# FFN ends of a two-layer encoder: the next norm's first rows turned by a DMA, product 2's weights kept for product 3, one activation split moved

## The chip, the core and the metric

The kernel runs on one core of a Trainium2 chip. The engines that it uses are TensorE (PE; its weight loads are PEld), VectorE (DVE), ScalarE (ACT), GpSimd (POOL) and SyncE (SP). SP issues the plain and the transposing DMAs, POOL the accumulating ones; each engine works through its own queue in order. The metric is the device time of one execution in microseconds (us).

## The reference

A residual stream x of 512 tokens by 1024 features in float32 goes through two layers and a last norm:

```python
for l in range(DEPTH):      # 2
    x = x + 0.5 * swiglu(rms_norm(x, ffn1_norm[l]), ffn1_w_in[l], ffn1_w_out[l])
    x = x + mixer(rms_norm(x, mix_norm[l]), mix_w_in[l], ...)
    x = x + 0.5 * swiglu(rms_norm(x, ffn2_norm[l]), ffn2_w_in[l], ffn2_w_out[l])
return rms_norm(x, final_norm)

def rms_norm(x, g): return x * rsqrt(mean(x * x, -1) + 1e-6) * g
def swiglu(x, w_in, w_out):
    g, u = split(x @ w_in, 2, axis=-1)      # w_in 1024 x 5632
    return (silu(g) * u) @ w_out            # w_out 2816 x 1024
```

The mixer (neighbourhood attention beside a 2-D Fourier transform, gated) is not touched by the change. There are four FFNs: FFN1 and FFN2 of layer 0, FFN1 and FFN2 of layer 1. Their ends, in order of time, are called ends 1 to 4. The last one is followed by the final norm and not by another stage.

## The kernel before

**Products.** Every large product is done by one level of Strassen's scheme: both matrices are cut into 2 by 2 blocks, and seven products of sums of blocks, numbered 1 to 7, take the place of eight. Each float32 operand is split into a high part of reduced precision (type fp32r) and the rest, its low part, and each term of a product is three matmuls in `product` and `granule`: high weights by high activations (L508), high by low (L509), low by high (L511). One matmul takes a 128x128 weight block against 128x512 values.

**Weights.** They come from memory as granules of 128 x 1024 float32 (512 KB; 256 KB for 128 x 512). `Raw.load` issues one load on SP (L148); where a granule is a sum of two blocks, POOL adds a second one in place by an accumulating DMA (L150). The granules lie in a pool of 9 buffers. On the chip each is split: ScalarE copies it to `whi` (L186 or L191), VectorE subtracts that from it to give `wlo` (L187 or L194), three buffers of each. `Stream` runs over the list of all granules in order of use: loads are issued up to 8 items ahead of the split (`FETCH`), the split is made 2 items ahead of its use (`AHEAD`). Product 3 needs the sum of blocks d and b: its item loads d, with its accumulate, and b again, and VectorE adds the two (`Item.summed`, L164) ahead of the split.

**The body of an FFN** (`stage_ffn`) does gate and up products over five blocks of the hidden features. A block does products 1, 5, 6, 2, 7, 3 and 4 in that order into the PSUM tiles A, B and C. From them come two halves of gated values, z2 and then z1 (z2 before product 4, z1 behind it). They have tokens on the partitions and must be turned: `halves` calls `apart`, in which ScalarE makes two copies that separate the 16-bit words of z (tile `zs`, L346) and SP issues one transposing DMA to tile `zt` (L347). Later ScalarE joins the words again (`joined_words`, L356), two instructions per z, into the activation tiles `at`. For the last block that happens inside the FFN end.

**The FFN end** is the loop over `steps`: 21 short products against the output weights, i = 0 to 20, each over one of three chunks c of hidden features. Product 1 is i = 0 to 2, product 2 is i = 3 to 5, then chunk by chunk products 5, 6, 7 and 3 (i = 6 to 17), and product 4 (i = 18 to 20). Chunk 0 has three blocks of 128 hidden features per half (18 matmuls), chunks 1 and 2 have four (24 matmuls). `make(i)` splits the activations of step i: for product m, ScalarE makes the tile `c<m>h` and VectorE `c<m>l` (L321, L322). The program calls `make` for steps i, i + 1 and i + 2 around step i. z1 of the last block is joined behind i = 2, z2 behind i = 5. Finished sums are added into x by VectorE (`update`, L756).

**The next norm** needs its rows of x turned and split into tiles `xh` and `xl` (two buffers each). For the first quarter, `nxt.quad(0, 0)` behind i = 6, TensorE transposes eight 128x128 blocks into PSUM (L413), ScalarE takes them out with the norm's gain (L416) and makes the high half (L417), and VectorE makes the low half (L418). From the end of the block loop, where the FFN's own norm tiles have had their last use, until those tiles are written anew, `xh` and `xl` lie unused. In end 4 (`late`) there is no next norm of this kind.

The order of the instructions in each engine's queue is laid out when the kernel is built, by a planner that works from the program's order and the engines' modelled loads; in a few places, around i = 18 among them, it is written out by hand (`manual_schedule`).

Of the kernel before, what the change touches and what calls it, by code (L numbers as in the profile page):

```python
# [9 lines left out]
F32 = mybir.dt.float32  # L10
# [3 lines left out]
U16 = mybir.dt.uint16  # L14
AF = mybir.ActivationFunctionType
# [3 lines left out]
P = 128  # L19
D = 1024  # L20
T = 512
# [16 lines left out]
NB = 5  # L38
# [52 lines left out]
def encoder_kernel(  # L91
# [45 lines left out]


    class Raw:
        def __init__(self, key, n=1024, plus=None):  # L140
            self.key, self.n, self.plus, self.t = key, n, plus, None

        def load(self, parts=1):
            if self.t is None:
                self.t = raw_pool[0](self.n)
                for c in range(0, self.n, self.n // parts):
                    cs = slice(c, c + self.n // parts)
                    nc.sync.dma_start(out=self.t[:, cs], in_=wst[GRAN_AT[self.key]][:, cs])  # L148
                if self.plus:
                    G.dma_start(out=self.t, in_=wst[GRAN_AT[self.plus]][:, 0 : self.n], accum_op=ALU.add)  # L150
# [48 lines left out]
    def stage_items():  # L199
        items, st = [], 0  # L200

        def add(*a, **k):
            items.append(Item(*a, stage=st, **k))

        def strassen(s, name, idx, sizes, order, dma=False, behind=None):
            def key(q, g):
                return (s, name(q), idx, g) if g < 2 else (s, "h" + q, idx, 0)

            r = {}
            for q, q2 in (("a", None), ("b", None), ("c", "a"), ("d", "c")):  # L210
                r[q] = [Raw(key(q, g), n, q2 and key(q2, g)) for g, n in enumerate(sizes)]
            d2 = [Raw(key("d", g), n) for g, n in enumerate(sizes)]
            at = [(m, g) for m in order for g in range(len(sizes))]
            if len(sizes) == 3:
                at.remove((2, 2))
                at.insert(at.index((7, 2)), (2, 2))
            for m, g in at:
                a, b, c, d = [r[q][g] for q in "abcd"]
                if m == 1:
                    add(a, neg=True)  # L220
                elif m == 2:
                    add(b)
                elif m == 3:
                    add(d, None if dma else b)
                elif m == 4:
                    add(d2[g])
                elif m == 5:
                    add(d)
                elif m == 6:
                    add(d, a, then=b.key if dma else None)  # L230
                else:
                    add(c)
                for key in (behind or {}).get(m, ()) if g == len(sizes) - 1 else ():
                    add(Raw(key))

        def out_sizes(c):
            return (1024, 512) if c == 0 else (1024, 1024)

        def ffn(s):
            first = not items  # L240
            if first:
                for g in range(4):
                    add(Raw((s, "cl", g)), parts=2 if g < 2 else 1, pieces=2 if g == 0 else 1)
            for j in range(NB):
                order = (1, 2, 5, 6, 7, 3, 4) if first and j == 0 else (1, 5, 6, 2, 7, 3, 4)
                strassen(s, lambda q: q, j, (1024,) * (2 if first or j else 3), order)
            for order in ((1,), (2,), (5, 6, 7, 3), (4,)):
                for c in range(3):
                    strassen(s, lambda q: "o" + q, c, out_sizes(c), order)

        for l in range(L):
            ffn((l, 1))
            st += 1
# [12 lines left out]
            for g in range(2):  # L266
                add(Raw((s, "n", 1, g)))
            strassen(s, lambda q: "w" + q, 0, two, ORDER, True)
            ffn((l, 2))
        return items  # L270

    class Stream:
# [6 lines left out]
        def fetch(self, to):  # L279
            n = len(self.items)  # L280
            while self.loaded < min(to, n) and self.items[self.loaded].stage <= self.stage:
                self.items[self.loaded].load()
                self.loaded += 1

# [25 lines left out]

    ws = Stream()
    raw_pool = [None]

    def mm3(ps, lh, ll, rh, rl, start, stop, again=False):
        PE.matmul(ps, lh, rh, start=start, stop=False, skip_group_check=again)  # L315
# [15 lines left out]
    def rsqrt(ms, n):  # L331
# [6 lines left out]
            V.scalar_tensor_tensor(r, t, 1.5, r, ALU.add, ALU.mult)  # L338
        return r

    def apart(z):

        s, t = slot(U16, "zs", (2, 4, 2, P)), slot(U16, "zt", (2, 4, 256))
        words = z.bitcast(U16).rearrange("p b (q f h) -> p h q b f", q=4, h=2)
        for h in range(2):
            S.activation(s[:, h], words[:, h], AF.Copy)  # L346
        nc.sync.dma_start_transpose(  # L347
            out=t.rearrange("p h q (b t) -> p (h q b) t", b=2), in_=s.rearrange("p h q b f -> p (h q b f)")
        )
        return t  # L350

    def joined_words(to, t):

        to = to.bitcast(U16).rearrange("p i (t w) -> p w i t", w=2)
        for w in range(2):
            S.activation(to[:, w], t[:, w], AF.Copy)  # L356

    class Norm:
# [39 lines left out]

        def quad(self, i, j):
            self.quad_high(i, j)()  # L400

        def quad_high(self, i, j):

# [211 lines left out]
    def stage_ffn(norm, nxt, late):  # L615
# [77 lines left out]
        def halves(z, j, f0):  # L693

            turned.append((apart(z), j, f0))
# [175 lines left out]
        for jb in range(0 if first else 1, NB):  # L871
# [36 lines left out]
            z2 = gate(s2, 1)  # L908
            times(z2, [sb[:, 0, :], sb[:, 1, :]], 1)
            halves(z2, 1, f0)  # L910
            product(pa, acts[4], K4, False, again=True)
            times(z1, pa, 0)
            halves(z1, 0, f0)

        if late or nxt.mix:
            tc.keep_in_program_order(S.activation(small("sq", 1), ones, AF.Sqrt))
        ps = {}
        for i, (m, c, _) in enumerate(steps):
            make(i)
            if i:  # L920
# [1067 lines left out]
```

## Time and profile before

| | |
|---|---|
| three runs | 1858.85, 1858.40, 1857.83 us, median 1858.4 |
| profiled execution | 1859.64 us, span 1857.9 us |
| granted TensorE clock, mean | 0.999 |
| TensorE busy | 1842.2 us (99%), 8862 matmuls |
| VectorE busy | 1605.6 us (86%) |
| ScalarE busy | 1311.2 us (71%) |
| GpSimd busy | 171.3 us (9%) |
| DMA traffic | 394.21 MB, 212 GB/s over the span |
| SP's weight loads of 512 KB | 470, 5.7 us from issue to landing (median) |
| POOL's accumulates of 512 KB | 174, 8.0 us |
| SP's transposing DMAs | 44, 5.5 us |

In the lines below, a timeline row reads: start in us, length in us, engine, line of the kernel, operation, tile written <- tiles read, shape and type, count; in brackets the idle time of that engine before it and what ended it. Matmuls overlap, so the distance between starts, not the length, is what one costs.

### The profile page before, as it was taken

What the parts mean: (1) busy time and instruction counts of PE and PEld (TensorE: products, weight loads), DVE (VectorE), ACT (ScalarE), POOL (GpSimd) and SP (SyncE); (2) the same over time, 40 slices, a digit from 0 to 9 for tenths busy, and PEclk for the clock granted to TensorE, in tenths of its full rate; (3) what the DMA queues carried; (4) which work ended last, traced back from release to release, by engine and by line L of the source; (5) the groups of instructions that cost most, each with busy time, mean ns of one, the idle gap of its engine ahead of it and who ended that gap; (6) DMA issues with size and microseconds to landing.
All of it is one profiled execution on the core that took longest, in us unless ns stands there. A gap on an engine that the chain in (4) does not pass through costs nothing.

```text
span 1857.9 us, 24616 instructions
## 1 busy us (share of the span) xinstructions
PE 1842.2 (99%) x8862; PEld 1530.1 (82%) x8862; DVE 1605.6 (86%) x1950; ACT 1311.2 (71%) x1780; POOL 171.3 (9%) x210
## 2 busy tenths in 40 slices
PE   9999999999999999999999999999999999999997
PEld 7888878888888888888888888888888888888886
DVE  7878899786889987889998888998869899887898
ACT  6777875668676767777666778766675776777865
POOL 0001011100111010001010100101001101010010
PEclk9999999999999999999999999999999999999999
DMA  9898799932896788879888887988249867888794
GB/s 301 222 240 219 188 255 277 216 118 86 248 230 183 180 224 223 216 199 263 253 200 217 225 216 198 268 278 212 69 150 237 227 174 178 234 210 215 211 280 145
DMA packets 198458, 394.21 MB, mean 212 GB/s; under 512 B 103808, under 2 KB 103936, under 8 KB 198336
## 3 DMA queue, kind: packets, MB, share of 16 engines
q1 hardware_dynamic: 169664, 294.30, 49.2%
q0 software_dynamic: 28528, 98.33, 29.7%
q8 instruction: 69, 1.13, 0.3%
q14 instruction: 53, 0.43, 0.1%
q10 hardware_dynamic: 144, 0.02, 0.0%
HBM read 365.85 MB, written 2.11 MB: 198 GB/s over the span
## 4 chain that ended last, share of the span: by engine, by line
PE 88%; DVE 6%; DMA 2%; issue 2%; ACT 1%; SPq 0%; DVEq 0%; ACTq 0%
PE A L508 10%; PE A L511 10%; PE A L509 10%; PE B L509 5%; PE B L508 5%; PE B L511 5%; PE o L511 5%; PE o L509 5%; PE o L508 4%; PE ps L315 4%; PE ps L316 3%; PE ps L317 3%; PE C L508 3%; PE C L509 3%; PE C L511 3%
## 5 line engine op out<-in xcount | busy, mean ns | idle before, releaser
L194 DVE TENSOR_TENSOR wlo<-raw,whi 128x1024 fp32r<-128x1024 f32 (+1 forms) x534 | 632.0, 1195 | 172.8 <-ACT whi L191 171.3
L191 ACT ACTIVATE whi<-raw 128x1024 fp32r<-128x1024 f32 (+1 forms) x534 | 546.0, 1033 | 253.5 <-DVE raw L164 56.9
L150 POOL DMA_DIRECT2D raw<-in_wst_dram x166 | 144.2, 887 | 1339.3 <-DMA raw<-in_wst_dram 596.8
L164 DVE TENSOR_TENSOR raw<-raw,raw 128x1024 f32<-128x1024 f32 (+1 forms) x150 | 179.2, 1195 | 2.0
L509 PE MATMUL A<-whi,xl 128*128 128x512 f32 x400 | 155.7, 389 | 0.0
L508 PE MATMUL A<-whi,xh 128*128 128x512 f32 x400 | 155.7, 389 | 0.0
L356 ACT ACTIVATE at<-zt 128x1024 uint16<-128x1024 uint16 (+2 forms) x96 | 111.0, 1168 | 20.9 <-DMA zt<-zs 20.9
L186 ACT ACTIVATE whi<-raw 128x1024 fp32r<-128x1024 f32 (+1 forms) x83 | 85.9, 1035 | 46.9 <-issue 12.5
L511 PE MATMUL A<-wlo,xh 128*128 128x512 f32 x400 | 115.0, 389 | 0.0
L187 DVE SCALAR_TENSOR_TENSOR wlo<-raw,whi 128x1024 fp32r<-128x1024 f32 (+1 forms) x83 | 98.4, 1195 | 11.3 <-ACT whi L186 11.0
L511 PEld LDWEIGHTS A<-wlo,xh 128*128 128x128 f32 x400 | 75.1, 188 | 15.6
L508 PEld LDWEIGHTS A<-whi,xh 128*128 128x128 f32 x400 | 75.1, 188 | 15.4
L509 PEld LDWEIGHTS A<-whi,xl 128*128 128x128 f32 x400 | 75.1, 188 | 15.4
L508 PE MATMUL C<-whi,xh 128*128 128x512 f32 x208 | 81.1, 390 | 0.5 <-ACT whi L191 0.5
L509 PE MATMUL C<-whi,xl 128*128 128x512 f32 x208 | 81.0, 389 | 0.0
L509 PE MATMUL B<-whi,xl 128*128 128x512 f32 x208 | 81.0, 389 | 0.0
L508 PE MATMUL B<-whi,xh 128*128 128x512 f32 x208 | 80.9, 389 | 0.0
L730 ACT ACTIVATE th<-sn,rh 128x512 f32<-128x512 f32 x80 | 55.1, 715 | 36.2 <-DVE sn L583 35.4
L346 ACT ACTIVATE zs<-th 128x1024 uint16<-128x1024 uint16 x80 | 79.5, 1042 | 0.9 <-DVE th L737 0.9
L578 ACT ACTIVATE sn<-A 128x512 f32<-128x512 f32 x104 | 59.0, 584 | 24.9 <-PE A L511 24.9
L511 PE MATMUL B<-wlo,xh 128*128 128x512 f32 x208 | 59.8, 389 | 0.0
L511 PE MATMUL C<-wlo,xh 128*128 128x512 f32 x208 | 59.8, 389 | 0.0
(438 smaller groups left out, 4681.5 us busy)
## 6 DMA issues: line engine op xcount, KB each, us to landing
raw<-in_wst_dram SPq DMA_DIRECT2D x470, 512.0 KB, 5.7
raw<-in_wst_dram POOLq DMA_DIRECT2D x174, 512.0 KB, 8.0
raw<-in_wst_dram SPq DMA_DIRECT2D x30, 256.0 KB, 3.8
bm<-in_bias_dram SPq DMA_DIRECT2D x16, 384.0 KB, 3.5
x<-in_xin_dram SPq DMA_DIRECT2D x4, 512.0 KB, 10.2
raw<-in_wst_dram POOLq DMA_DIRECT2D x8, 256.0 KB, 8.4
dft<-in_dft_dram POOLq DMA_DIRECT2D x8, 256.0 KB, 4.3
gb<-in_gbias_dram SPq DMA_DIRECT2D x4, 512.0 KB, 14.8
```

The lines of the kernel that those rows point to most:

```text
L150: G.dma_start(out=self.t, in_=wst[GRAN_AT[self.plus]][:, 0 : self.n], accum_op=ALU.add)
L164: V.tensor_tensor(self.raw.t, self.raw.t, self.add.t, ALU.add)
L186: S.activation(hi, t, AF.Copy, scale=-1.0)
L187: self.last = V.scalar_tensor_tensor(lo, t, -1.0, hi.bitcast(F32), ALU.mult, ALU.subtract)
L191: S.activation(hi[:, cs], t[:, cs], AF.Copy)
L194: self.last = V.tensor_tensor(lo[:, cs], t[:, cs], hi[:, cs].bitcast(F32), ALU.subtract)
L315: PE.matmul(ps, lh, rh, start=start, stop=False, skip_group_check=again)
L346: S.activation(s[:, h], words[:, h], AF.Copy)
L356: S.activation(to[:, w], t[:, w], AF.Copy)
L508: PE.matmul(ps, lh, rh, start=start, stop=False, skip_group_check=again)
L509: PE.matmul(ps, ll, rh, start=False, stop=False, skip_group_check=again)
L511: PE.matmul(ps, lh, rl, start=False, stop=stop, skip_group_check=again)
```

## The change

It touches the four FFN ends in three ways.

1. Product 2's granules (block b) get a fixed home. They are loaded into `kept[0]` and `kept[1]`, which are two tiles of the tag `xh`, and `kept[2]`, one of tag `xl`, and the same data serve product 3, so b is not loaded a second time: five loads of 512 KB and one of 256 KB fewer per end, 24 loads over the kernel. The stream's loading stops at such an item until `homes[0]` is set behind the block loop. In the built order of SP's queue, the kept loads stand among the other loads around the last block's two transposing DMAs: between that of z2 and that of z1 there is one load of 512 KB in the kernel before, and there are two of 512 KB and one of 256 KB in the changed one. Kept tile 2 is one that the last block's product 3 reads last (its low activations), kept tile 0 another of product 3 (the high ones), kept tile 1 one that product 4 reads.
2. In ends 1 to 3, `nxt.quad(0, 0)` is replaced by the generator `turned_quad`, advanced one step behind each of i = 6, 8, 11, 12, 13, 14 and 15: two ScalarE copies of words of x into tile `words` (the other `xl` tile), a transposing DMA on SP, two joins, four scalings by the gain, and the split. TensorE's eight transposes per end go away.
3. `make(2)`, the activation split of the third chunk of product 1, is called in the last block ahead of its product 4 and no longer behind i = 0.

```diff
     class Raw:
-        def __init__(self, key, n=1024, plus=None):
-            self.key, self.n, self.plus, self.t = key, n, plus, None
+        def __init__(self, key, n=1024, plus=None, home=None):
+            self.key, self.n, self.plus, self.home, self.t = key, n, plus, home, None
         def load(self, parts=1):
             if self.t is None:
-                self.t = raw_pool[0](self.n)
+                self.t = homes[0](*self.home, self.n) if self.home else raw_pool[0](self.n)
...
+            if kept:
+                r["b"] = kept
...
+            kept = [
+                [Raw((s, "ob", c, g), n, home=(c, g)) for g, n in enumerate(out_sizes(c))] for c in range(3)
+            ]
             for order in ((1,), (2,), (5, 6, 7, 3), (4,)):
                 for c in range(3):
-                    strassen(s, lambda q: "o" + q, c, out_sizes(c), order)
+                    strassen(s, lambda q: "o" + q, c, out_sizes(c), order, kept=kept[c])
...
         def fetch(self, to):
             while self.loaded < min(to, n) and self.items[self.loaded].stage <= self.stage:
+                if self.items[self.loaded].raw.home and not homes[0]:
+                    break
...
+        def turned_quad(self, i, j, st):
+
+            js = slice(j * 256, (j + 1) * 256)
+            s = st[:, 0].rearrange("p (h q b f) -> p h q b f", h=2, q=4, b=2)
+            t = st[:, 1].rearrange("p (h q c) -> p h q c", h=2, q=4)
+            words_apart(x[:, 2 * j : 2 * j + 2, i * T : (i + 1) * T], s)
+            yield
+            turned_words(s, t)
+            yield
+            raw = self.raw[i, j] = slot(F32, "xr")
+            for w in range(2):
+                joined_words(raw, t, (w,))
+                yield
+            self.tiles(i)
+            for k in range(4):
+                S.activation(raw[:, k, :], raw[:, k, :], AF.Copy, scale=self.gain(4 * i + k))
+                if k % 2:
+                    yield
+            split(self.h[i][:, :, js], self.l[i][:, :, js], raw)
+            yield
...
             halves(z2, 1, f0)
+            if jb == NB - 1:
+                make(2)
             product(pa, acts[4], K4, False, again=True)
...
         ps = {}
+        kept = [np_.tile([P, 4, T], F32, tag="xh", name=nm("ob"), bufs=2) for _ in range(2)]
+        words = np_.tile([P, 2, 2048], U16, tag="xl", name=nm("zq"), bufs=2)
+        kept.append(np_.tile([P, 4, T], F32, tag="xl", name=nm("ob"), bufs=2))
+        homes[0] = lambda c, g, n: kept[c][:, 2 * g : 2 * g + n // T, :].rearrange("p k t -> p (k t)")
+        quad00 = nxt.turned_quad(0, 0, words)
         for i, (m, c, _) in enumerate(steps):
...
             make(i + 2)
-            if i == 6 and not late:
-                nxt.quad(0, 0)
+            if i == 6:
+                homes[0] = None
+            if i in (6, 8, 11, 12, 13, 14, 15) and not late:
+                next(quad00)
```

`apart` is cut into `words_apart` (the copies) and `turned_words` (the DMA), and `joined_words` takes which of the two words to join; both do for z what they did.

More of the change, by code (lines that the diff above doesn't have):

```diff
@@ L203, in add, with strassen @@
             items.append(Item(*a, stage=st, **k))
-        def strassen(s, name, idx, sizes, order, dma=False, behind=None):
+        def strassen(s, name, idx, sizes, order, dma=False, behind=None, kept=None):
             def key(q, g):
@@ L312, in encoder_kernel @@
     raw_pool = [None]
+    homes = [None]
     def mm3(ps, lh, ll, rh, rl, start, stop, again=False):
@@ L339, in rsqrt, with words_apart @@
         return r
-    def apart(z):
-        s, t = slot(U16, "zs", (2, 4, 2, P)), slot(U16, "zt", (2, 4, 256))
+    def words_apart(z, s):
         words = z.bitcast(U16).rearrange("p b (q f h) -> p h q b f", q=4, h=2)
@@ L346, in apart, with turned_words @@
             S.activation(s[:, h], words[:, h], AF.Copy)
+    def apart(z):
+        s, t = slot(U16, "zs", (2, 4, 2, P)), slot(U16, "zt", (2, 4, 256))
+        words_apart(z, s)
+        return turned_words(s, t)
+    def turned_words(s, t):
         nc.sync.dma_start_transpose(
@@ L350, in apart, with joined_words @@
         return t
-    def joined_words(to, t):
+    def joined_words(to, t, ws=(0, 1)):
         to = to.bitcast(U16).rearrange("p i (t w) -> p w i t", w=2)
-        for w in range(2):
+        for w in ws:
             S.activation(to[:, w], t[:, w], AF.Copy)
```

## The prediction

> **What bounds the kernel now.** I read the page's busy shares first, then the DMA queues.
>
> ```profile
> PE 1842.2 (99%) x8862; PEld 1530.1 (82%) x8862; DVE 1605.6 (86%) x1950; ACT 1311.2 (71%) x1780; POOL 171.3 (9%) x210
> q1 hardware_dynamic: 169664, 294.30, 49.2%
> q0 software_dynamic: 28528, 98.33, 29.7%
> ```
>
> TensorE is 99% busy over the span of 1857.9 us, so a change pays only where TensorE waits, or by taking work from it. Both can happen in this change at one place, the four FFN ends (an FFN's last 21 short products, i = 0 to 20). The view of busy time by window, from the start of product i = 3 to that of i = 18 in each end, shows what is special there (columns: window, length, then busy time and count per engine, clock, DMA share, GB/s):
>
> ```profile
> 236.50:314.50 78.00, 77.37 (x339) 62.31 (x338) 76.37 (x79) 52.18 (x65) 10.02 (x12) 1.00 0.93 268
> 838.17:913.88 75.71, 75.71 (x338) 62.45 (x337) 74.15 (x76) 49.53 (x62) 8.60 (x10) 1.00 0.92 263
> 1158.16:1234.68 76.52, 76.20 (x339) 62.61 (x338) 75.75 (x79) 50.60 (x63) 9.14 (x12) 1.00 0.93 268
> 1758.33:1833.16 74.83, 74.83 (x331) 61.95 (x330) 73.78 (x77) 47.94 (x57) 8.63 (x10) 1.00 0.91 261
> ```
>
> VectorE (third busy figure: 76.37 of 78.00, 74.15 of 75.71, 75.75 of 76.52, 73.78 of 74.83) is as full as TensorE. The two run neck and neck, and whichever ends last sets when product 4 (i = 18) starts. The timeline of TensorE gives each end's zero (first matmul of i = 0) and the first matmul of i = 18:
>
> ```profile
> 220.55 0.39 PE L508 MATMUL o<-whi,c1h 128*128 128x512 f32 x1
> 821.71 0.39 PE L508 MATMUL o<-whi,c1h 128*128 128x512 f32 x1
> 1142.20 0.39 PE L508 MATMUL o<-whi,c1h 128*128 128x512 f32 x1
> 1742.35 0.39 PE L508 MATMUL o<-whi,c1h 128*128 128x512 f32 x1
> 314.51 0.40 PE L508 MATMUL o<-whi,c4h 128*128 128x512 f32 x1
> 1833.16 0.39 PE L508 MATMUL o<-whi,c4h 128*128 128x512 f32 x1
> ```
>
> With the middle two starts from the windows above (913.88, 1234.68), the stretch takes 93.96, 92.17, 92.48 and 90.81 us.
>
> What sets VectorE's pace inside it? Its queue stands still early on, until the second activation transpose (zt of z1) has landed; from c2l 128x1024 (the low half for i = 4, whose high half c2h stands behind that transpose's joins in ScalarE's queue) onward it runs back to back, but for one late gap. ScalarE's joins of zt, then VectorE's c2l, then that gap:
>
> ```profile
> 235.85 1.37 ACT L356 ACTIVATE at<-zt 128x1024 uint16<-128x1024 uint16 x1 [3.14 <-DMA zt<-zs]
> 834.56 1.38 ACT L356 ACTIVATE at<-zt 128x1024 uint16<-128x1024 uint16 x1 [1.79 <-DMA zt<-zs]
> 1155.66 1.37 ACT L356 ACTIVATE at<-zt 128x1024 uint16<-128x1024 uint16 x1 [1.31 <-DMA zt<-zs]
> 1755.08 1.38 ACT L356 ACTIVATE at<-zt 128x1024 uint16<-128x1024 uint16 x1 [0.58 <-DMA zt<-zs]
> ...
> 240.06 1.21 DVE L322 TENSOR_TENSOR c2l<-at,c2h 128x1024 fp32r<-128x1024 f32 x1
> 838.60 1.23 DVE L322 TENSOR_TENSOR c2l<-at,c2h 128x1024 fp32r<-128x1024 f32 x1 [0.86 <-ACT c2h L321]
> 1159.88 1.22 DVE L322 TENSOR_TENSOR c2l<-at,c2h 128x1024 fp32r<-128x1024 f32 x1
> 1759.31 1.22 DVE L322 TENSOR_TENSOR c2l<-at,c2h 128x1024 fp32r<-128x1024 f32 x1
> ...
> 281.83 1.23 DVE L194 TENSOR_TENSOR wlo<-raw,whi 128x1024 fp32r<-128x1024 f32 x1 [0.42 <-ACT whi L191]
> 881.19 1.23 DVE L194 TENSOR_TENSOR wlo<-raw,whi 128x1024 fp32r<-128x1024 f32 x1 [1.10 <-PE o L511]
> 1202.01 1.23 DVE L194 TENSOR_TENSOR wlo<-raw,whi 128x1024 fp32r<-128x1024 f32 x1 [0.77 <-ACT whi L191]
> 1801.73 1.23 DVE L194 TENSOR_TENSOR wlo<-raw,whi 128x1024 fp32r<-128x1024 f32 x1 [1.05 <-ACT whi L191]
> ```
>
> In all four ends ScalarE was idle for that DMA. Counted from zero, the landing (start of the join) is at 15.3, 12.9, 13.5 and 12.7 us, and c2l starts at 19.5, 16.9, 17.7 and 17.0: 4.0 to 4.2 us behind the landing.
>
> **The change, part by part.** First what it takes away from TensorE: eight transposes per end in three ends.
>
> ```profile
> 256.35 1.03 PE L413 MATMUL tr<-ident,x 128*128 128x128 f32 x8
> 257.14 0.48 PE L508 MATMUL o<-whi,c6h 128*128 128x512 f32 x1
> 257.45 0.39 PE L509 MATMUL o<-whi,c6l 128*128 128x512 f32 x1
> 257.68 0.40 PE L508 MATMUL o<-whi,c6h 128*128 128x512 f32 x1
> ...
> PE o L509 <- DVE c1l L322: 1.6, 3, 0.5
> PE o L508 <- ACT c2h L321: 1.0, 1, 1.0
> ...
> 1828.90 1.22 DVE L194 TENSOR_TENSOR wlo<-raw,whi 128x1024 fp32r<-128x1024 f32 x1
> ```
>
> From the first transpose to the second matmul behind it are 257.45 − 256.35 = 1.10 us, of which one matmul's pace (257.68 − 257.45 = 0.23) remains: 0.87 us, three times, 2.6 us of TensorE work. Second, make(2), moved ahead of the last block's product 4, gives VectorE c1l two places earlier; by the list of waits (us, times, us each) the stalls on c1l, three ends of 0.5, go, and the fourth end's, on c2h, 1.0, may: 2.6 us. These 5.2 us are all that TensorE could give, and they pay only where VectorE comes as much earlier.
>
> VectorE's work from c2l to i = 17 is the same number of instructions: the kept weights of product 2 are still split and still added once for product 3 (L164), and the low half of the norm's first rows (L418) moves from about i = 9 to i = 17, inside the stretch. So the shift at i = 18 is the shift of c2l, less the late gap that a queue running later no longer has (0.42, 1.10, 0.77, 1.05). In end 4 there is slack besides: the last low half of weights ends at 1830.12, and TensorE takes it at 1831.35, so 1.2 us.
>
> So everything hangs on when zt of z1 lands. The transposing DMAs and the weight loads are all issued by SP's queue:
>
> ```profile
> 223.64 4.95 SPq L347 DMA_TRANSPOSE zt<-zs  x1
> 228.68 0.53 SPq L148 DMA_DIRECT2D raw<-in_wst_dram  x1
> 229.30 3.47 SPq L347 DMA_TRANSPOSE zt<-zs  x1
> 824.79 3.49 SPq L347 DMA_TRANSPOSE zt<-zs  x1
> 828.37 0.53 SPq L148 DMA_DIRECT2D raw<-in_wst_dram  x1
> 829.00 3.55 SPq L347 DMA_TRANSPOSE zt<-zs  x1
> DMA to landing us min/median/max: 4.3/5.5/8.9
> ...
> 237.08 0.60 ACT L191 ACTIVATE whi<-raw 128x512 fp32r<-128x512 f32 x1
> ```
>
> Before, one load of 512 KB stands between the two transposes. After, in SP's built order, two and a half do (the second granule of a kept weight, one of 256 KB, one of 512 KB). Before the first transpose stand the other kept loads, which could not be issued until the dead tiles came free (two with the last block's product 3, one with its product 4), so SP waits there, and everything queued behind it with it; POOL's two accumulating DMAs for product 3's d weights now run at the same time.
>
> The price of those bytes comes from the DMA queues: 294.30 MB in 49.2% of 1857.9 us is 1.63 us per 512 KB load; 98.33 MB in 29.7% is 2.94 us per accumulate. Two and a half loads are 4.1 us. In end 1, SP is through with the first transpose at 228.6, 8.1 after zero; the loads follow, 4.1, and the second transpose behind them takes at least the shortest landing, 4.3: it lands at **16.5**. End 2 had SP free at 6.7 (828.37 − 821.71), which would give 15.1; but with five kept granules and one and a half accumulates (some 12 us of DMA time by the prices above, from 5.5 us before zero, as the last block's product 4 is 24 matmuls of 0.23) ahead, I take end 1's case for all. The lower end: only three issues in place of one, 1.25 us at 0.63 each, on end 2's 7.3, and the median landing 5.5: 14.0. The upper end: the same on end 1's 8.75 and the longest landing, 8.9: 18.9.
>
> From the landing to c2l: before, 4.2 us, with a 128x512 weight copy of ScalarE (0.60, the last row) between the two joins. After, that copy stands ahead of the joins, in the wait, so c2l comes 3.6 behind the landing, at 20.1. Shifts: end 1, 20.1 − 19.5 − 0.4 = +0.2; end 2, 20.1 − 16.9 − 1.1 = +2.1; end 3, 20.1 − 17.7 − 0.8 = +1.6; end 4, 20.1 − 17.0 − 1.05 − 1.2 = +0.9. Sum **+4.8 us**. At 14.0 the same sums give −2.3, −0.4, −0.9 and −0.5 (there TensorE's own stall is the limit): −4.1. At 18.9: +2.6, +4.5, +4.0, +3.3: +14.4. It breaks even near 15.3.
>
> A load just ahead does seem to count: from issue to landing the second transpose takes 6.5 us in end 1 (229.30 to 235.85) and 5.6 in end 2 (829.00 to 834.56), against 4.3 at best. The rule that bears on this: the Trainium skill, page "DMA: Bandwidth & Descriptors", section "Queues, rings and completion order", says that SP owns one queue row, a ring on each of the 16 DMA engines, and that on each engine descriptors are consumed in ring order, so that a transpose issued behind loads stands behind them. By that rule the sum is +4.8; if SP's later issue alone counted, −4.1.
>
> The other edits. The 24 loads that fall away (six per end, 5.5 granules, 9 us of DMA time at 1.63) lie in the stretch where DMA engines are 91 to 93% busy but no engine's row waits for a load; I cost them at nothing, and below that nothing, because VectorE, not DMA, is full there. The turned quad adds to ScalarE, per end, two copies (1.04 each), two joins (1.37) and four scalings instead of four from PSUM: about 5 us in a stretch where it is busy 52 of 78; its transpose is issued about product i = 8, and in the built order its joins stand behind the weight copies of i = 14, which are made two products ahead: four products of 4.1 to 5.4 us (18 and 24 matmuls), about 18 us, against a longest landing of 8.9. Were that cover gone, it would cost what it lands late, in three ends. The added wait on SP (dead tiles) holds up the loads behind it, whose first use is some products on. Product 4, the mixers and the tail (TensorE idle behind the last product) keep their instructions; behind i = 17 TensorE leads, so the shift stays.
>
> The profiled execution itself took 1859.64 us, 1.7 above the span and 1.2 above the median of the three runs, 1858.4; the sum against it is 1864.4, and on the median 1858.4 + 4.8 = **1863.2**.
>
> **The rivals.** A, faster: zt of z1 lands by 14 after all, because loads and transposes overlap on the 16 DMA engines. For it: in end 2 it landed 5.6 us behind its issue, near the median, with a load just ahead. Against: end 1, and DMA shares over 0.9. It decides below 14.1; price −4.1, 1854.3, and at most the 5.2, 1853.2. B, nothing measurable: it lands between 14.1 and 16.2, as end 2's own issue times give (15.1); the saved transposes and stalls are eaten where VectorE is late. At 15.1 the four shifts are −1.3, +0.7, +0.1 and −0.5: 1857.4. C, worse: besides, the weights queued behind SP's wait for dead tiles come late, or the turned quad's joins stand in ScalarE's queue ahead of weight copies before their DMA has landed; at the upper landing, 1872.8. For it: SP's queue is strictly in order; against: 18 us of cover.
>
> **How the numbers follow.** Forecast (landing 16.2 to 18.9) 0.49, its own range 1862 to 1872; A 0.17, B 0.28, C 0.06. Within 0.2% (3.7 us, about what a measurement of this kernel can tell from no change) is B. The range, 1854.5 to 1871.0, leaves out most of A and the upper end with C.
>
> **What would show it.** In the changed profile: ScalarE's first join behind zt of z1 at about 16.5 after zero, with idle for that DMA growing from 3.14/1.79/1.31/0.58 in every end; c2l 3.6 us behind it; no stall on c1l; 24 transposes fewer on TensorE; i = 18 at 94.1, 94.3, 94.1 and 91.7 after zero. I am wrong if the landing is at 14 or less, if VectorE's queue is no longer back to back between c2l and i = 17, or if a new wait of TensorE outside these stretches carries the difference.

## The result and the profile after

The changed kernel takes 1871.07 us (median of six runs, 1870.71 to 1871.58) against 1858.12 us before (six runs, 1857.06 to 1860.60): the ratio is 1.0068, 95% interval 1.0057 to 1.0079. It is slower, as forecast, but by 12.9 us and not by 4.8, level with the upper end of the range (1871.07 against 1871.0; the six runs spread over 0.87 us). The profiled execution took 1871.03 us, 11.4 more than that of before, with a span of 1869.1 us. The page's busy times and DMA queues:

```profile
PE 1843.8 (99%) x8838; PEld 1529.1 (82%) x8838; DVE 1604.7 (86%) x1950; ACT 1324.1 (71%) x1792; POOL 171.4 (9%) x210
q1 hardware_dynamic: 172448, 284.33, 48.0%
q0 software_dynamic: 28528, 98.33, 29.5%
```

TensorE has its 24 transposes fewer, and SP's queue moves 10 MB less; neither makes the kernel faster. The timeline of ScalarE shows the joins that wait for zt of z1, that of VectorE the c2l behind them, that of TensorE the first matmul of i = 4, all in ends 1 to 4:

```profile
236.66 1.36 ACT L372 ACTIVATE at<-zt 128x1024 uint16<-128x1024 uint16 x1 [4.45 <-DMA zt<-zs]
840.33 1.35 ACT L372 ACTIVATE at<-zt 128x1024 uint16<-128x1024 uint16 x1 [5.98 <-DMA zt<-zs]
1163.17 1.36 ACT L372 ACTIVATE at<-zt 128x1024 uint16<-128x1024 uint16 x1 [4.94 <-DMA zt<-zs]
1767.87 1.37 ACT L372 ACTIVATE at<-zt 128x1024 uint16<-128x1024 uint16 x1 [5.03 <-DMA zt<-zs]
...
240.15 1.23 DVE L330 TENSOR_TENSOR c2l<-at,c2h 128x1024 fp32r<-128x1024 f32 x1 [4.59 <-ACT c2h L329]
843.80 1.23 DVE L330 TENSOR_TENSOR c2l<-at,c2h 128x1024 fp32r<-128x1024 f32 x1 [6.09 <-ACT c2h L329]
1166.66 1.22 DVE L330 TENSOR_TENSOR c2l<-at,c2h 128x1024 fp32r<-128x1024 f32 x1 [5.08 <-ACT c2h L329]
1771.35 1.23 DVE L330 TENSOR_TENSOR c2l<-at,c2h 128x1024 fp32r<-128x1024 f32 x1 [5.17 <-ACT c2h L329]
...
241.12 0.50 PE L545 MATMUL o<-whi,c2h 128*128 128x512 f32 x1 [1.87 <-ACT whi L191]
844.76 0.61 PE L545 MATMUL o<-whi,c2h 128*128 128x512 f32 x1 [3.37 <-ACT whi L191]
1167.63 0.50 PE L545 MATMUL o<-whi,c2h 128*128 128x512 f32 x1 [2.36 <-ACT whi L191]
1772.32 0.50 PE L545 MATMUL o<-whi,c2h 128*128 128x512 f32 x1 [2.45 <-ACT whi L191]
```

The ends now start at 220.05, 822.19, 1146.07 and 1750.67, so the landing is at 16.6, 18.1, 17.1 and 17.2 us after zero and c2l at 20.1, 21.6, 20.6 and 20.7. The wait that took the place of the old ones is the same join: TensorE runs out of work at i = 4 and stands 1.9 to 3.4 us for the weight copy that ScalarE makes behind it. Then the view by window, from c2l to the start of i = 18 (314.09, 917.74, 1240.59, 1845.09):

```profile
240.15:314.09 73.94, 72.06 (x313) 58.28 (x313) 73.94 (x76) 53.29 (x65) 8.59 (x11) 1.00 0.83 230
843.80:917.74 73.94, 72.97 (x313) 59.66 (x314) 73.94 (x76) 53.65 (x65) 6.31 (x8) 0.98 0.76 204
1166.66:1240.59 73.93, 72.05 (x313) 58.28 (x314) 73.93 (x76) 53.28 (x65) 6.82 (x8) 1.00 0.84 232
1771.35:1845.09 73.74, 72.77 (x312) 59.68 (x313) 73.74 (x77) 47.25 (x56) 6.88 (x8) 0.98 0.70 189
```

VectorE is busy for every microsecond of it in all four ends, as the forecast had it. In ends 1 to 3 its last low half of weights also ends just before TensorE takes it; in end 4 that is ready 2.3 us early (it ends 90.3 us after zero and is taken at 92.6), so there TensorE itself sets i = 18. i = 18 starts 94.0, 95.6, 94.5 and 94.4 us after zero, against 94.0, 92.2, 92.5 and 90.8 before: +0.1, +3.4, +2.0 and +3.6, together 9.1 of the 11.2 us between the two spans.

Two rows of these windows show a clock of 0.98. Cut finer, behind the two longest stalls:

```profile
844.80:848.40 3.60, 3.60 (x9) 2.79 (x10) 3.60 (x5) 3.48 (x4) 0.86 (x1) 0.53 1.05 279
848.40:852.00 3.60, 3.60 (x18) 2.98 (x17) 3.60 (x4) 3.53 (x4) 0.00 (x0) 1.00 1.09 216
...
1774.00:1777.00 3.00, 3.00 (x9) 2.32 (x8) 3.00 (x4) 3.00 (x5) 0.86 (x1) 0.53 1.07 270
1777.00:1780.00 3.00, 3.00 (x15) 2.48 (x14) 3.00 (x4) 2.94 (x3) 0.00 (x0) 1.00 1.10 216
```

For some 3.4 us TensorE is granted half its clock: a matmul costs 0.43 us there in place of 0.23.

The rest of the span's difference lies outside the ends: 2.4 us at the start of mixer 1 (between ends 3 and 4), 0.9 between ends 1 and 2, where mixer 0 lies, −0.5 at the start of the program and −0.7 in the tail. Mixer 1's has rows of its own. ScalarE's first copy of a summed weight there, then the POOL queue, of the changed kernel:

```profile
1261.27 1.06 ACT L191 ACTIVATE whi<-raw 128x1024 fp32r<-128x1024 f32 x1 [3.68 <-DMA raw<-in_wst_dram]
...
1249.89 0.56 POOL L1100 DMA_DIRECT2D ch<-in_chan_dram  x1 [36.66 <-DMA bm<-in_bias_dram]
1250.43 1.77 POOL L150 DMA_DIRECT2D raw<-in_wst_dram  x2
```

and of the kernel before:

```profile
1230.97 0.56 POOL L1054 DMA_DIRECT2D ch<-in_chan_dram  x1 [17.64 <-DVE wlo L194]
1236.86 0.85 POOL L150 DMA_DIRECT2D raw<-in_wst_dram  x1 [5.33 <-PE o L509]
```

The mixer's channel matrix, `ch`, is loaded into memory of the FFN's granule buffers. With six granules fewer per end, the rotation of the 9 buffers has moved on, and in mixer 1 that memory now belongs to a late granule of the FFN: by the program's waits, `ch` waits for the low half of a granule that VectorE makes shortly before 1249 (the row above names the bias load instead; in run 2 below, as before the change, the row names the low half). In POOL's queue the mixer's first two accumulates stand behind it and come 13.6 us later in the span than before, of which the late ends make up some 6.

### The profile page after: what moved, and what is told of

Its sections match the earlier page's. It is cut to its first block, busy times and chain, and to the rows that moved or that the text cites. A ratio compares the mean times of both kernels' runs of the same rounds, so it can differ in the third digit from the quotient of the medians.

```text
span 1869.1 us, 24504 instructions
## 1 busy us (share of the span) xinstructions
PE 1843.8 (99%) x8838; PEld 1529.1 (82%) x8838; DVE 1604.7 (86%) x1950; ACT 1324.1 (71%) x1792; POOL 171.4 (9%) x210
## 4 chain that ended last, share of the span: by engine, by line
PE 89%; DVE 4%; DMA 3%; issue 2%; ACT 1%; SPq 0%; DVEq 0%; POOL 0%; POOLq 0%; ACTq 0%
PE A L545 10%; PE A L548 10%; PE A L546 10%; PE o L548 5%; PE o L545 5%; PE o L546 5%; PE B L546 5%; PE B L545 5%; PE B L548 5%; PE ps L323 4%; PE ps L324 3%; PE ps L325 3%; PE C L545 3%; PE C L546 3%; PE C L548 3%
## 5 line engine op out<-in xcount | busy, mean ns | idle before, releaser
L194 DVE TENSOR_TENSOR wlo<-raw,whi 128x1024 fp32r<-128x1024 f32 (+1 forms) x510 | 603.0, 1193 | 165.4 <-ACT whi L191 165.0
L191 ACT ACTIVATE whi<-raw 128x1024 fp32r<-128x1024 f32 (+1 forms) x510 | 522.4, 1035 | 245.3 <-DVE raw L164 64.5
L164 DVE TENSOR_TENSOR raw<-raw,raw 128x1024 f32<-128x1024 f32 x126 | 151.4, 1203 | 2.0
L186 ACT ACTIVATE whi<-raw 128x1024 fp32r<-128x1024 f32 (+1 forms) x83 | 85.8, 1034 | 45.6 <-PE A L546 13.9
L546 PEld LDWEIGHTS A<-whi,xl 128*128 128x128 f32 x400 | 75.1, 188 | 15.5
```

The source lines that it names most:

```text
L164: V.tensor_tensor(self.raw.t, self.raw.t, self.add.t, ALU.add)
L186: S.activation(hi, t, AF.Copy, scale=-1.0)
L191: S.activation(hi[:, cs], t[:, cs], AF.Copy)
L194: self.last = V.tensor_tensor(lo[:, cs], t[:, cs], hi[:, cs].bitcast(F32), ALU.subtract)
L546: PE.matmul(ps, ll, rh, start=False, stop=False, skip_group_check=again)
```

## The experiments

The theory: zt of z1 lands late because of where SP's queue has it, and everything in the ends follows from that; mixer 1's loss is POOL's queue, separately. The rivals: the bytes of the burst (bandwidth), wherever they stand in the queue; and ScalarE's or VectorE's added work.

**1. zt of z1 ahead of the loads.** Loads of `kept[1]`'s second granule, and plain loads from the fourth on, are queued behind the transposing DMA:

```diff
...
+                held = ahead_of[0] and (self.home in ((1, 1),) if self.home else others[0] > 3)
+                with tc.issue_after(ahead_of[0].ins) if held else nullcontext():
...
                     nc.sync.dma_start(out=self.t[:, cs], in_=wst[GRAN_AT[self.key]][:, cs])
```

> The changed kernel with one difference: the second transposing DMA (zt of z1) is issued right behind the first, ahead of the two and a half loads that stood before it. Queue theory (the loss in the FFN ends comes from those loads standing ahead of it): it lands 2.5 x 1.63 = 4.1 us earlier, at about 12.5, 14.0, 13.0 and 13.1 us after zero in ends 1 to 4; no stall of TensorE at i = 4, no half clock behind it; i = 18 starts 3.9, 0.4, 2.0 and 0.5 us earlier than in the kernel before; mixer 1 still loses its 2.4 us; about 1853.5 us. Rival, bandwidth (the burst of kept loads and accumulates ahead of both transposes makes them late, wherever the last loads stand): landing moves by less than 1 us and the time stays within 3 us of 1871.

Measured: 1855.80 us against 1859.08, ratio 0.9980 (0.9971 to 0.9990). ScalarE's joins, ends 1 to 4 (zeros at 220.00, 819.17, 1138.89, 1740.51):

```profile
233.62 2.58 ACT L376 ACTIVATE at<-zt 128x1024 uint16<-128x1024 uint16 x2 [1.44 <-DMA zt<-zs]
831.97 1.37 ACT L376 ACTIVATE at<-zt 128x1024 uint16<-128x1024 uint16 x1 [2.46 <-DMA zt<-zs]
1151.95 1.38 ACT L376 ACTIVATE at<-zt 128x1024 uint16<-128x1024 uint16 x1 [0.89 <-DMA zt<-zs]
1753.31 2.60 ACT L376 ACTIVATE at<-zt 128x1024 uint16<-128x1024 uint16 x2 [0.63 <-DMA zt<-zs]
```

The landing is at 13.6, 12.8, 13.1 and 12.8, the stall at i = 4 is gone, and i = 18 starts 1.8, 0.8, 2.0 and 0.7 us earlier than before the change. The same work, with one DMA moved past three others in its queue, is some 15 us faster than the change as it was made. In the sum over the kernel it stays 2 us short of the 1853.5 expected: end 1 gained 1.8 us in place of 3.9, as its landing came 1.1 us later than expected and TensorE waited 1.8 us for one of VectorE's low halves 88 us after zero. The mixer's loss stayed (3.4 us between ends 3 and 4 in this profile).

**2. ch behind the accumulates.**

```diff
-        G.dma_start(out=ch, in_=chan)
+        with tc.issue_after(last_sum[0].ins):
+            G.dma_start(out=ch, in_=chan)
```

> The changed kernel with one difference: the mixers' load of their channel matrix (tile ch) is queued on POOL behind the mixer's first two accumulates instead of ahead of them. POOL theory (in mixer 1, ch waits for the buffer of the last FFN granule and holds up the accumulates behind it, for which ScalarE and TensorE wait): the 3.7 us idle of ScalarE before whi in mixer 1 goes, the 2.4 us between end 3 and end 4 go, the four ends stay as they are: about 1868.7 us. Rival (those accumulates are late because the DMA engines are behind): their sums land as late as now, time within 1 us of 1871.

Measured: 1868.14 us, ratio 1.0053 (1.0038 to 1.0068). POOL's queue at mixer 1:

```profile
1236.46 0.86 POOL L150 DMA_DIRECT2D raw<-in_wst_dram  x1 [24.07 <-ACT whi L191]
1237.73 0.86 POOL L150 DMA_DIRECT2D raw<-in_wst_dram  x1 [0.41 <-issue]
1249.59 0.56 POOL L1102 DMA_DIRECT2D ch<-in_chan_dram  x1 [10.99 <-DVE wlo L194]
```

`ch` still waits 11 us for the low half of that granule, but nothing waits behind it; ScalarE's idle time and the shift at mixer 1 are gone. The second cause stands, at about 2.8 us. Run 3 below ties it to the kept weights: with them alone the stretch between ends 3 and 4 is 3.3 us longer than before, and with the turned quad alone (run 4) it is not longer.

**3 and 4. One part alone.** The kept weights without the rest, and the turned quad without the rest (each the kernel before with that part's lines of the diff).

> The kernel before with the kept weights alone: TensorE's transposes and make(2) as before. In its built order one load of 512 KB stands between the two transposing DMAs, as in the kernel before, and four and a half kept and plain loads ahead of the first. Queue theory: zt of z1 lands 1.5 x 1.63 = 2.4 us earlier than in the changed kernel, at 14.2 to 15.7 us after zero, the stall at i = 4 is under 1 us, and the ends together lose 0 to 3 us against the kernel before; with mixer 1's 2.4 us, 1858 to 1864 us. Bandwidth rival: landing as in the changed kernel, 16.6 to 18.1, and a time above 1867.

> The kernel before with the turned quad alone: product 2's weights are loaded again for product 3, make(2) stands where it stood. SP's order around the two zt transposes is that of the kernel before. Queue theory with VectorE as the limit up to i = 17: landing as before (15.3, 12.9, 13.5, 12.7), the 2.6 us of transposes taken off TensorE hardly show, because VectorE ends as late: 1857 to 1858.5 us. Rival (TensorE is the limit in these ends): the whole 2.6 us come off, 1855.5. Rival (ScalarE's extra copies and joins cost): slower than 1860.

Measured: kept weights alone 1865.94 us, ratio 1.0041 (1.0027 to 1.0055); zt of z1 lands at 16.8, 14.1, 15.5 and 13.7, stalls up to 1.2 us. In end 1 the landing came as the bandwidth rival had it, in the others as the queue theory had it or earlier; in end 1 the burst ahead of the first transpose held SP for 6.5 us (run 8 takes that burst away). The time is 2 us above my upper figure, but not for the ends: in the profile they lose 1.2 us together, mixer 1 loses 3.3, and 0.9 goes between ends 1 and 2.

The turned quad alone is the surprise: 1875.95 us, ratio 1.0097 (1.0075 to 1.0119), worse than the whole change. zt lands as before (15.2 in end 1), but the turned quad's own transposing DMA, issued 36 to 38 us after zero, lands 9.2 to 18.1 us later, and then TensorE waits up to 4.8 us for weights. DMA traffic in end 2 around it (issued at 864.07):

```profile
860.00:864.00 4.00, 4.00 (x19) 3.30 (x18) 4.00 (x7) 3.94 (x9) 0.85 (x1) 1.00 0.78 285
...
868.00:872.00 4.00, 4.00 (x19) 3.34 (x18) 4.00 (x5) 1.18 (x3) 0.00 (x0) 1.00 1.34 72
872.00:876.00 4.00, 4.00 (x19) 3.30 (x19) 4.00 (x5) 2.79 (x3) 0.00 (x0) 1.00 1.53 101
876.00:880.00 4.00, 2.33 (x11) 1.59 (x9) 2.08 (x2) 0.00 (x0) 0.00 (x0) 1.00 0.91 102
...
881.99 1.06 ACT L191 ACTIVATE whi<-raw 128x1024 fp32r<-128x1024 f32 x1 [7.20 <-DMA raw<-in_wst_dram]
```

The DMA engines count as full, at a share of 0.91 to 1.53, and move 72 to 102 GB/s in place of 285. ScalarE, whose added copies and joins were a rival, stands idle for 7.2 us there (last row): it waits for a weight to land, so its own work is not what costs the time. What sets this run apart from the changed kernel is the place of POOL's accumulates: here two were issued within 2.4 us ahead of that DMA or just with it, there none until 1.0 us or more behind it, where it landed in 4.3 to 7.4 us.

**5. Both repairs together** (1 and 2).

> Both repairs in the changed kernel: zt of z1 issued right behind zt of z2, and ch queued behind the mixer's first accumulates. If the two losses are separate causes, the gains add: 1855.8 less the 2.6 us that mixer 1 still lost with the first repair alone (2.9 measured for the second alone), so 1853.0 us, faster than the kernel before by 5 us. Rival (mixer 1's loss only showed because the end before it ran late): no gain on 1855.8.

Measured: 1851.28 us, ratio 0.9962 (0.9948 to 0.9976). The gains add: run 1 took 0.0088 off the changed kernel's ratio and run 2 took 0.0015, which gives 0.9965.

**6. make(2) alone.**

> The kernel before with make(2) alone moved ahead of the last block's product 4. In its built order one and a half loads stand between the two transposing DMAs, in place of one. The stall on c1l goes (1.6 us over three ends as listed), but VectorE sets i = 18; zt of z1 lands about 0.8 us later (half a load), so the ends shift by -1 to +0.8 us each: 1857 to 1861 us. Rival (TensorE sets the end): 1857.4 less 1.6 to 2.9, under 1856.5.

Measured: 1857.70 us, ratio 0.9994 (0.9983 to 1.0005): nothing. zt of z1 landed at 14.5, 15.5, 15.0 and 14.4, and the ends changed by −2.0, +0.2, −0.6 and +0.2 us in the profile: end 1, where it landed earlier than before, gained, and in the others the later landing took back what the earlier c1l brought. The half load is not what made it late. ScalarE now makes make(2)'s high half ahead of z1's copies, which end 9.05 us after zero in place of 7.06, and the transposing DMA is issued at 9.07 in all four ends; in end 2 SP was through with the loads at 7.6.

**7. Filler for the clock.**

```diff
+            if i == 4:
+                idle = bank("idle")
+                for _ in range(16):
+                    tc.keep_in_program_order(PE.transpose(idle[:, 0:P], ident, ident))
```

> The changed kernel with sixteen 128x128 transposes of the identity put on TensorE ahead of product i = 4, about 1.8 us of work that nobody reads, where TensorE sat idle 1.9 to 3.4 us. Clock theory (an idle of 2.4 us or more is followed by some 3 us at half the granted clock; VectorE hides it in end 2, not in end 4): no window of half clock behind i = 4, end 4 shorter by 1.7 to 1.9 us, the other ends within 0.5 us, 1869.3 us. Rival (the slow matmuls have another cause than the idle): the matmuls behind i = 4 stay at 0.43 us in ends 2 and 4, 1871.

Measured: 1876.04 us, ratio 1.0091 (1.0077 to 1.0105). The clock is as the theory has it, at 1.00 behind the filler; around i = 4 (first matmul at 1776.34) in end 4:

```profile
1773.00:1776.00 3.00, 3.00 (x23) 2.71 (x21) 0.63 (x1) 3.00 (x4) 1.11 (x2) 1.00 1.04 311
1776.00:1779.00 3.00, 2.93 (x14) 1.99 (x13) 3.00 (x4) 3.00 (x4) 0.61 (x1) 1.00 1.03 270
```

But the added instructions also made the planner lay out VectorE's and ScalarE's queues behind i = 4 in another order, and TensorE then waited eleven times, 8.1 us in all, for low halves of weights. The time says nothing of the clock's price.

**8. The burst thinned too.** As 5, with `self.home in ((1, 0), (1, 1), (2, 0), (2, 1))`: ahead of the transposes stay the plain loads and kept tile 0.

> As the run with both repairs, but the loads of kept tiles 1 and 2 are queued behind zt of z1 as well; ahead of the transposes stay the plain loads and kept tile 0. Bandwidth rival (the burst ahead makes the transposes slow): zt of z1 lands another 1 to 2 us earlier, near 12 us after zero, and the ends gain 1 to 3 us more, 1850 to 1852 us. Queue theory with the transposes' issue set by their copies: landing within 0.7 us of the run with both repairs and a time within 1 us of it; a loss if kept tile 1 comes too late for i = 4 (needed near 15 us after zero).

Measured: **1848.22 us, ratio 0.9943 (0.9929 to 0.9956)**, the fastest of all, 10.6 us below the kernel before by that ratio. The signs of the bandwidth rival came: zt of z1 lands at 11.8 in all four ends, 0.7 to 2.0 us earlier than in run 5 and ahead of its join in three, and the first transposing DMA holds SP for 2.0 to 2.9 us in place of 5.1 to 6.5. So the loads between the transposes count (run 1) and those ahead of both as well. ScalarE and VectorE have the same work here as in the changed kernel, so their added work was not the cause either. From the start of each end to i = 18, by window, and TensorE's list of waits over the whole program:

```profile
220.00:309.76 89.76, 89.76 (x397) 74.38 (x396) 89.70 (x93) 69.57 (x82) 10.88 (x13) 1.00 0.94 263
817.15:907.58 90.43, 90.27 (x397) 74.23 (x396) 89.56 (x93) 67.91 (x80) 8.63 (x10) 1.00 0.84 233
1135.92:1225.68 89.76, 89.76 (x398) 74.34 (x397) 89.70 (x93) 69.58 (x82) 10.35 (x12) 1.00 0.93 263
1732.58:1822.34 89.76, 89.76 (x397) 74.35 (x396) 89.70 (x94) 62.79 (x73) 8.63 (x10) 1.00 0.79 222
...
PE ps L136 <- DVE ones L132: 1.2, 1, 1.2
PE o L553 <- DVE wlo L197: 0.2, 1, 0.2
```

89.76 us is what 396 matmuls take at 0.2267 us: the ends run at TensorE's pace (end 2 takes 0.7 us more), and there is nothing left to take from their waits.

**9, 10, 11. The parts again, with the landing repaired.** 9 is run 8 with TensorE's transposes in place of the turned quad; 10 the kernel before with make(2) and zt of z1 first, no kept weights; 11 the same with the turned quad.

> As the fastest run so far (both repairs, kept tiles 1 and 2 loaded behind zt of z1), but with TensorE's eight transposes per end and without the turned quad. In that run TensorE set the pace of all four ends (89.76 us, no wait), so now the transposes should cost what they take: 3 x 0.87 = 2.6 us, 1850.8 us. Rival (VectorE still hides them): within 0.7 us of 1848.2. Rival (the turned quad costs more in DMA than it saves): below 1847.5.

> The kernel before with make(2) moved and zt of z1 issued right behind zt of z2, no kept weights and no turned quad. If the gain of the fastest run comes from the early landing of zt of z1 alone, this has most of it: landing near 12 to 13 us after zero, ends 1.5 to 3 us shorter each but for the transposes' 0.87, 1851 to 1854 us. Rival (the 24 loads saved are what makes room): no better than 1856.

> The same with the turned quad in place of the transposes on TensorE, still without kept weights. Collision theory (in the run with the turned quad alone, its transposing DMA met two of POOL's accumulates, and DMA traffic fell to 72 to 150 GB/s for some 12 us, so weights came late): it lands 9 us or more after its issue in ends 1 to 3, TensorE stalls there on whi for several us, over 1862 us. Rival (that loss came from the old order around zt of z1): it lands within 6 us, no stall over 1 us, 1849 to 1851 us.

Measured: 1850.62 us (0.9959, 0.9945 to 0.9974), 1853.98 us (0.9972, 0.9962 to 0.9982) and 1883.71 us (1.0144, 1.0105 to 1.0183). So with the landing repaired the transposes cost 2.4 us by the medians where TensorE leads (2.1 in the profiles: ends 1 to 3 take 90.67 in place of 89.76 or 90.43), an early landing and make(2) give about 5 us by themselves, and the turned quad without the kept weights is worse still. Its DMA in run 11, end 2, was issued at 860.40 and landed 22.7 us later:

```profile
864.00:868.00 4.00, 4.00 (x20) 3.30 (x19) 4.00 (x6) 1.31 (x2) 0.00 (x0) 1.00 1.35 81
868.00:872.00 4.00, 4.00 (x19) 3.32 (x18) 4.00 (x5) 2.13 (x2) 0.00 (x0) 1.00 1.33 60
872.00:876.00 4.00, 2.68 (x12) 1.88 (x10) 1.02 (x1) 0.00 (x0) 0.00 (x0) 1.00 1.31 52
876.00:880.00 4.00, 0.00 (x0) 0.00 (x0) 0.00 (x0) 0.00 (x0) 0.00 (x0) 0.96 1.13 64
```

**12. Is it the adding?**

```diff
-                    G.dma_start(out=self.t, in_=wst[GRAN_AT[self.plus]][:, 0 : self.n], accum_op=ALU.add)
+                    how = {} if self.key[1:3] == ("od", 1) else {"accum_op": ALU.add}
+                    G.dma_start(out=self.t, in_=wst[GRAN_AT[self.plus]][:, 0 : self.n], **how)
```

> As the run before (turned quad, make(2), zt of z1 first, no kept weights), with the same instructions in the same order, but the two POOL DMAs ahead of the turned quad's transposing DMA (block d of chunk 1) overwrite in place of adding, with as many bytes written; the sums of these weights, and so the output, lack a block. Accumulate theory (what slows everything for some 12 to 20 us is a transposing DMA behind accumulating ones in flight): it lands within 6.5 us of its issue, TensorE's stalls of 4 to 9 us on whi go, 1849 to 1854 us. Bandwidth theory (too many bytes at that place, whatever their kind): it still lands 9 us or more behind its issue, above 1870 us.

Measured: 1860.83 us, ratio 1.0006 (0.9991 to 1.0021), 22.9 us less than run 11. The landing of the turned quad's DMA, first of run 11, then of run 12:

```profile
DMA to landing us min/median/max: 9.0/9.7/22.7
```

```profile
DMA to landing us min/median/max: 6.2/6.2/16.0
```

In ends 2 and 3, where both POOL DMAs were issued ahead of the transposing one, it lands in 6.2 us: there the accumulating was most of the trouble. In end 1 it took 16.0, where the second POOL DMA, plain now, was issued 0.5 us behind the transposing one. So the kind of DMA is not all of it, and neither theory holds as I put it. The moment goes with the worst cases in all three runs: wherever one of POOL's DMAs was issued 0.0 to 0.5 us behind the transposing one, that one took 16.0 to 22.7 us and the two landed within 0.7 us of each other (end 2 of runs 4 and 11, end 1 of run 12); with two accumulates ahead it took 9.0 to 9.9 us, with two plain writes ahead 6.2. In the changed kernel and in runs 1, 2, 5, 7 and 8, 18 cases, none came just ahead and the nearest accumulate behind was 1.0 us away or more; there it took 4.3 to 7.4. No run moved the moment alone, so why the two slow each other down stays open.

## Why the prediction was right in sign and short in size

**What bounds the ends: right in ends 1 to 3.** VectorE was back to back from c2l to i = 18, and TensorE, with its transposes gone, still had to wait for VectorE's last low halves (0.85 us in ends 1 and 3); the transposes' cost showed (2.4 us) once TensorE led (runs 8 and 9).

**The landing: right in mechanism, short in three ends.** 16.5 was forecast, 16.6, 18.1, 17.1 and 17.2 came. End 1's case, taken for all, was the best of the four and not the typical one. The term that was too small is the time until SP is through with the first transposing DMA: that DMA held SP for 5.4 to 6.0 us (4.95 in end 1 before), so SP was free at 8.2 to 8.9 us after zero and not at 8.1. The second then landed 8.4 to 9.3 us later, against 4.1 + 4.3. Runs 1 and 8 show the cause: three loads moved in SP's queue gave back 3.0 to 5.3 us of landing, and the thinned burst 1 to 1.8 more. The Trainium skill's rule on ring order (page "DMA: Bandwidth & Descriptors", section "Queues, rings and completion order"), which the prediction cites, fits both runs.

**From landing to c2l: right.** 3.5 us, 3.6 forecast. With the measured c2l, the shifts by the same sum are +0.2, +3.6, +2.1 and +1.5, together +7.4; measured +0.1, +3.4, +2.0 and +3.6, together +9.1.

**End 4: a term that was missing.** VectorE's slack of 1.2 us there was used up by TensorE itself. The stall at i = 4 ended 21.65 us after zero; 312 matmuls at 0.2267 us bring that to 92.4, and i = 18 started at 94.4. Of the 2.0 us between, 1.6 are eight matmuls at half clock, 0.43 us each. The prediction named no clock: the stall of 2.45 us at i = 4 was not in it, since it traced the late join to VectorE and not to the weight copy that TensorE needs behind it. In end 2 the same half clock lay beside VectorE's longer delay.

**The mixers "keep their instructions": true, and wrong as an argument.** The instructions were the same; the memory of one of them was not. The price, 2.4 us in the profile and 2.8 by run 2, was in no term. It is also the prediction's own sign of being wrong, a new wait of TensorE outside the ends, come in part. The 0.9 us between ends 1 and 2 I can't explain; over the profiles of all runs that stretch takes 507.0 to 508.6 us, so it may be no effect of the change.

**That the time lies at the range's edge: luck.** With the landings that came, the prediction's sum is +7.4 us; the profile shows 11.3. The rest came from the clock in end 4 and from mixer 1, which the range did not count on: its upper part stood for a landing at 18.9, and that did not come.

**The loads saved, costed at nothing: not what the runs say.** What they are worth in the change as it was made no run shows; run 9, with them, is 3.4 us below run 10, without them, but its landing is also 1.3 to 1.8 us earlier. Without them the turned quad's DMA met POOL's accumulates, and what I called 18 us of cover was gone (runs 4 and 11: zq landed up to 22.7 us after its issue). Whether the kept weights help there by their bytes or by moving the accumulates some 1 to 2 us behind that DMA is not settled.

**The rivals.** A, the early landing, was refuted for the change as it was made, though runs 1, 5 and 8 are that rival brought about by hand, and runs 5 and 8 gained more than its 5.2 us limit. That limit summed the listed waits and the transposes; the right one was in the prediction's own rows. In its fourth window, TensorE is busy throughout and does the 330 matmuls from i = 3 to i = 17 in 74.83 us, 0.2267 each, so an end's 396 take 89.8 us; the ends took 369.4 us together, and four times 89.76 is 359.0, so 10.4 us were to be had. C's mechanism (late weights, late turned quad) did not occur, though the time came out near C's.

## What to carry to other kernels

Before a change adds loads to a queue that also carries a latency-critical transfer, read the built order of that queue: the place of a few loads and of one small transfer in two queues is all that separates 1871 us from 1848. A saved buffer or load also shifts every later rotation of the same buffers; look for transfers of the next stage that land in that memory, and for what is queued behind them. And when one part of a change is costed at nothing, take it away by itself: here the saved loads were what kept the turned quad from costing some 17 us (run 4).

## What the runs showed of the hardware

In the changed kernel, TensorE's granted clock fell to half for some 3.4 us after TensorE had stood still for 2.45 and 3.37 us, and not after 1.87 and 2.36 us; with filler in the gap (run 7) it stayed at 1.00. The length of the pause does not decide it, though. Behind a pause of 2.78 us in end 3 of run 2 (until 1167.31) the clock stayed at 1.00, and behind one of 1.82 us in end 1 of run 11 (until 312.48) it fell. By window, around the pause in end 4 of the changed kernel, in run 2 and in run 11:

```profile
1770.01:1773.42 3.41, 1.10 (x4) 0.86 (x5) 2.07 (x3) 3.41 (x5) 0.94 (x2) 1.00 1.03 286
1773.42:1776.84 3.42, 3.42 (x9) 2.63 (x8) 3.42 (x4) 3.42 (x5) 0.86 (x1) 0.50 1.04 268
...
1162.50:1165.90 3.40, 2.03 (x9) 1.34 (x8) 0.00 (x0) 3.04 (x3) 0.86 (x1) 1.00 0.89 247
1165.90:1169.30 3.40, 1.99 (x8) 1.42 (x8) 2.95 (x4) 3.40 (x5) 0.86 (x1) 1.00 1.05 267
...
309.69:313.10 3.41, 1.59 (x8) 1.00 (x7) 3.41 (x4) 1.69 (x2) 0.00 (x0) 1.00 0.95 383
313.10:316.51 3.41, 3.41 (x10) 2.67 (x9) 3.41 (x6) 3.11 (x7) 1.06 (x2) 0.50 1.03 419
```

These windows are not chosen freely: within each trace here the granted clock changes only at times that lie whole multiples of 3.41 us apart (845.00, 848.41, 1773.42 and 1776.84 in the changed kernel; from the first to the third are 272 steps of 3.4133 us). Cut on that grid, over all the traces of this case, every interval at full clock in which TensorE stood still for 1.81 us or more is followed by half clock, none with 1.69 us or less is, and between the two both occur. Run 2's pause of 2.78 us falls on two intervals, with about 1.4 us in each. So it is in part chance, by how a pause lies on that grid, whether it costs the clock, and so it was with end 4's 1.6 us. The Trainium skill, page "TensorE: Matmul & The Clock Gate", section "What's actually happening", puts the condition at an idle window of about 3.4 us; here an interval of that length that was idle for little more than half was enough.

With a transposing DMA of 512 KB and accumulating DMAs in flight at the same time, the traffic of all 16 engines fell from 285 to 72 GB/s in run 4, and to 52 in run 11, for 12 to 20 us, at a busy share mostly above 1. With plain DMAs of POOL's, one of them issued 0.5 us behind the transposing one, it fell to 86 GB/s in end 1 of run 12. With nothing of POOL's within 1.0 us of its issue, the same DMA landed in 4.3 to 7.4 us.
